# Seven block products in the first feed-forward, PSUM tiles of their own, and modulation columns spread over the stages

## The chip, the core and the metric

The kernel runs on one core of a Trainium2 chip. The metric is the device time of one execution in microseconds; the time of a kernel is the median of its runs. Engines are named as in the profile: PE is TensorE (matmuls), DVE is VectorE, ACT is ScalarE, POOL is GpSimd, and SP is the engine that issues most transfers.

## The reference

Two layers over 512 tokens of 1024 channels. Layer 0 mixes with a Fourier transform and a windowed attention, layer 1 with pooled averages. Each layer ends with a gated feed-forward of 22 x 128 = 2816 hidden units, and six modulation vectors of 1024 (shift, scale and gate of the mixer and of the feed-forward) come from the condition c.

```python
def ada_mod(cond, w, b):
    m = jax.nn.silu(cond) @ w + b
    return jnp.split(m[..., None, :], 6, axis=-1)

def swiglu(h, w1, w3, w2):
    return (jax.nn.silu(h @ w1) * (h @ w3)) @ w2

def reference(x, c, ctx, ...):
    h, hc = x, ctx
    for layer in range(DEPTH):
        sh1, sc1, g1, sh2, sc2, g2 = ada_mod(c, ada_w[layer], ada_b[layer])
        ...
        xn = modulate(rms_norm(h, norm_mix_g[layer]), sh1, sc1)
        y = even_mixer(...) if layer % 2 == 0 else pool_mix(...)
        h = h + g1 * y
        hn = modulate(rms_norm(h, norm_ffn_g[layer]), sh2, sc2)
        h = h + g2 * swiglu(hn, ffn_w1[layer], ffn_w3[layer], ffn_w2[layer])
    return rms_norm(h, final_g)
```

Everything is fp32.

## The kernel before

**Products.** A fp32 product is made from halves: each operand is split into a rounded high part and the rest, and `passes` issues three matmuls: high x high, low x high, high x low. The weights' high part is a copy on ScalarE (`w_h`, line 67 is the helper of all its operations), the low part a subtraction on VectorE (`w_l`, L155). `Stream` (`ws`) keeps the weights in order: a raw piece of 128 x 1024 (512 KB) is loaded by SP into one of four `raw` buffers, and split some pieces ahead of its use.

**A feed-forward** (`ffn`, once for each layer). The hidden units are 22 tiles of 128, in groups of 8, 8 and 6 (`GROUPS`). A tile gives `av`, the product of the activated half and the other half, which is then split into `ah` and `al`. After each group come 8 output chunks: chunk `dt` multiplies the group's tiles with a piece of w2 in a PSUM bank `w2_ps` of the pool `mm`, and VectorE adds it, gated, to `h`. Tile 0 of each feed-forward is made ahead of it (`Lead`).

**An ordinary tile** takes two weight pieces and gives 8 x 2 x 3 = 48 matmuls of 512 columns into a two-bank tile `h_ps` of the pool `ss`, which has two such tiles.

**A block tile** (`Quarters`) computes the same as a 2 x 2 product of blocks with seven block products instead of eight, by the Winograd form of Strassen's scheme: 7 x 4 x 3 = 84 matmuls of 256 columns. The stationary sides are the raw block a1 (`w_r`), the sums s12 and s34 (`s_f`, made by VectorE with adds of 512 columns) and a22; each is split into halves. The moving sides are the blocks of the normed input and four combinations `t`, made once for a feed-forward in `pieces`. A product is named by its moving side (b11, t1, t2, t3, b21, t4, b22). Products are summed in four quarters of 256 columns, r[0] to r[3], of one two-bank `h_ps` tile; several products add to the same quarter. After four products VectorE makes `x`, `v` and part of `c_q`; after all seven, one add of 512 columns (L986) reads two quarters of the tile at once into `c_q`, and `av` follows. `first` and `second` prepare the next tile's weights inside the present tile. The low part of a22 is made differently from the others: ScalarE writes the negative of the high part, and a GpSimd transfer adds the raw weights from memory to it (L939, 256 KB, `accum_op`).

Before, `QUARTERED` has no tile of the first feed-forward and tiles 4 to 21 of the second.

**Modulation columns.** A column of a modulation vector is a dot product of 128 x 1024 weights with the condition: SP loads 512 KB (`ada_r`, L212) into a buffer of the same `raw` ring as the weights, and VectorE multiplies and sums it (L219). `acol1` has 56 of them left for the first feed-forward: the gate columns of its own layer and all of the second layer. Three are made after each tile from tile 2 on.

**What sets the order.** The Tile framework's scheduler orders the instructions of each engine from the program's order and from when their inputs should be there. So what is written after a group can be issued before its end. Each engine then runs its list in order, waiting on semaphores. The eight PSUM banks are: `mm` 3, `fl` 1, `ss` 2 x 2.

## Time and profile before

| | before |
|---|---|
| median of 3 runs | 1002.17 us (1000.08 to 1002.96) |
| profiled execution | 998.42 us |
| its span | 996.6 us |
| mean granted TensorE clock | 0.995 |
| TensorE busy | 960.5 us in 5464 matmuls |
| VectorE busy | 679.7 us |
| ScalarE busy | 428.1 us |
| GpSimd busy | 42.4 us |

The profile is of one execution. Times in the trace count from the start of its span; the first feed-forward lies at some 250 to 600 us, the second at some 640 to 983 us. A row of a windows view gives a stretch, its length, and the busy time and number of instructions of each engine in it. A row of a timeline gives start, length, engine, line, output and inputs, and in brackets how long the engine was idle before it and what ended that. Small differences between the median and the profiled execution are the usual ones between executions of one program.

### The profile page before, as it was taken

How to read it: one execution, taken by the hardware profiler on the slowest of the kernel's cores; microseconds unless marked ns; L12 is line 12 of the kernel's file. 1: busy time of each engine (PE TensorE's matmuls, PEld its weight loads, DVE VectorE, ACT ScalarE, POOL GpSimd, SP SyncE). 2: the span in 40 equal slices, each digit the busy share in tenths (PEclk: the TensorE clock that was granted, in tenths of full speed). 3: DMA queues.
4: the chain of work that ended last, by engine and by line, in shares of the span. 5: the costliest groups of instructions: out<-in, count | busy, mean ns of one | idle time of the engine just before them, and what ended most of it. 6: DMA issues, size and time to landing. Idle time of an engine off the chain costs nothing.

```text
span 996.6 us, 13925 instructions
## 1 busy us (share of the span) xinstructions
PE 960.5 (96%) x5464; PEld 800.5 (80%) x5464; DVE 679.7 (68%) x1086; ACT 428.1 (43%) x689; POOL 42.4 (4%) x45
## 2 busy tenths in 40 slices
PE   4999999999999999999999999999999999999995
PEld 3766767676888888888888888789989999889984
DVE  5678577879867455565456398898565885657654
ACT  4568565454532222232223355654432544315531
POOL 1011011011000000000000001000000100000000
PEclk9999999999999999999999999999999999999997
DMA  9931211753577446665365323133441444413412
GB/s 338 345 106 32 106 48 64 237 182 127 188 256 256 165 149 213 221 219 189 109 219 197 118 105 103 33 92 99 143 144 43 141 124 138 148 43 109 114 32 85
DMA packets 47009, 143.98 MB, mean 144 GB/s; under 512 B 5728, under 2 KB 5856, under 8 KB 46944
## 3 DMA queue, kind: packets, MB, share of 16 engines
q1 hardware_dynamic: 44352, 138.38, 40.9%
q0 software_dynamic: 2592, 4.72, 2.9%
q8 instruction: 43, 0.70, 0.3%
q14 instruction: 22, 0.18, 0.0%
HBM read 140.98 MB, written 2.10 MB: 144 GB/s over the span
## 4 chain that ended last, share of the span: by engine, by line
PE 84%; DVE 9%; ACT 4%; issue 2%; DMA 0%; DVEq 0%; SPq 0%; ACTq 0%
PE h_ps L180 14%; PE h_ps L181 14%; PE h_ps L182 14%; PE w_ps L180 8%; PE w_ps L182 8%; PE w_ps L181 8%; PE pv_ps L757 2%; ACT w_h L67 2%; DVE w_l L155 2%; PE t_ps L746 2%; PE mo_ps L180 1%; PE mo_ps L182 1%; PE mo_ps L181 1%; PE s_ps L709 1%; PE s_cx L422 1%
## 5 line engine op out<-in xcount | busy, mean ns | idle before, releaser
L67 ACT ACTIVATE w_h<-w_r 128x1024 fp32r<-128x1024 f32 (+2 forms) x158 | 148.0, 942 | 276.4 <-PE h_ps L182 154.5
L180 PE MATMUL h_ps<-hnh,w_h 128*128 128x512 f32 (+1 forms) x600 | 212.0, 353 | 3.0 <-DVE c_q L986 2.9
L181 PE MATMUL h_ps<-hnh,w_l 128*128 128x512 f32 (+1 forms) x600 | 210.5, 351 | 0.4 <-DVE w_l L155 0.4
L182 PE MATMUL h_ps<-hnl,w_h 128*128 128x512 f32 (+1 forms) x600 | 210.5, 351 | 0.0
L155 DVE TENSOR_TENSOR w_l<-w_r,w_h 128x1024 fp32r<-128x1024 f32 (+2 forms) x140 | 158.6, 1137 | 57.8 <-ACT w_h L67 57.2
L219 DVE SCALAR_TENSOR_TENSOR ada_r<-ada_r,condB 128x1024 f32<-128x1024 f32 x80 | 97.5, 1221 | 69.4 <-DMA ada_r<-in_adaR_dram 68.9
L180 PE MATMUL w_ps<-ah,w_h 128*128 128x512 f32 x352 | 137.5, 391 | 0.0
L181 PE MATMUL w_ps<-ah,w_l 128*128 128x512 f32 x352 | 137.0, 389 | 0.0
L182 PE MATMUL w_ps<-al,w_h 128*128 128x512 f32 x352 | 136.8, 390 | 0.0
L180 PEld LDWEIGHTS h_ps<-hnh,w_h 128*128 128x128 f32 x600 | 113.3, 189 | 20.6 <-DVE c_q L986 4.8
L181 PEld LDWEIGHTS h_ps<-hnh,w_l 128*128 128x128 f32 x600 | 113.4, 189 | 15.9 <-DVE w_l L155 0.8
L182 PEld LDWEIGHTS h_ps<-hnl,w_h 128*128 128x128 f32 x600 | 113.4, 189 | 14.9
L1052 DVE SCALAR_TENSOR_TENSOR h<-w_ps,ada,h 128x512 f32<-128x512 f32 x48 | 35.7, 749 | 67.8 <-PE w_ps L182 67.8
L181 PE MATMUL h_ps<-t_h,w_l 128*128 128x256 f32 x288 | 81.5, 283 | 0.0
L180 PE MATMUL h_ps<-t_h,w_h 128*128 128x256 f32 x288 | 81.5, 283 | 0.0
L182 PE MATMUL h_ps<-t_l,w_h 128*128 128x256 f32 x288 | 81.5, 283 | 0.0
L180 PEld LDWEIGHTS w_ps<-ah,w_h 128*128 128x128 f32 x352 | 66.1, 188 | 14.7 <-ACT ah L67 1.3
L182 PEld LDWEIGHTS w_ps<-al,w_h 128*128 128x128 f32 x352 | 66.1, 188 | 14.2 <-DVE al L1031 0.6
L181 PEld LDWEIGHTS w_ps<-ah,w_l 128*128 128x128 f32 x352 | 66.1, 188 | 13.3
L67 ACT ACTIVATE w_h<-s_f 128x1024 fp32r<-128x1024 f32 x36 | 38.0, 1056 | 55.0 <-PE w_ps L182 31.5
L67 ACT ACTIVATE ah<-av 128x512 fp32r<-128x512 f32 x44 | 27.8, 632 | 67.4 <-DVE av L1028 47.4
L155 DVE TENSOR_TENSOR w_l<-s_f,w_h 128x1024 fp32r<-128x1024 f32 x36 | 44.1, 1225 | 17.3 <-ACT w_h L67 17.0
(271 smaller groups left out, 1536.3 us busy)
## 6 DMA issues: line engine op xcount, KB each, us to landing
w_r<-in_w_dram SPq DMA_DIRECT2D x88, 512.0 KB, 3.6
ada_r<-in_adaR_dram SPq DMA_DIRECT2D x80, 512.0 KB, 4.2
w_r<-in_w2a_dram SPq DMA_DIRECT2D x32, 512.0 KB, 4.2
ada_q<-in_adaP_dram SPq DMA_DIRECT2D x32, 256.0 KB, 5.7
w_r<-in_w2b_dram SPq DMA_DIRECT2D x16, 384.0 KB, 3.0
w_l<-in_w_dram POOLq DMA_DIRECT2D x18, 256.0 KB, 5.5
w_r<-in_wo_dram SPq DMA_DIRECT2D x16, 256.0 KB, 2.9
wa_r<-in_wa_dram SPq DMA_DIRECT2D x8, 384.0 KB, 6.0
```

Source lines behind the costliest of these rows:

```text
L67: return nc.scalar.activation(out=out, in_=in_, func=func, **kw)
L155: nc.vector.tensor_tensor(lo, src, f32(hi), op=ALU.subtract)
L180: nc.tensor.matmul(acc, wh, mh, start=start, stop=False, skip_group_check=shared)
L181: nc.tensor.matmul(acc, wl, mh, start=False, stop=False, skip_group_check=shared)
L182: nc.tensor.matmul(acc, wh, ml, start=False, stop=stop, skip_group_check=shared)
L219: nc.vector.scalar_tensor_tensor(out=r, in0=r, scalar=1.0, in1=condB, op0=ALU.mult, op1=ALU.mult, accum_out=ada[l][:, t:t + 1])
L422: nc.tensor.matmul(ps[32 * g:32 * g + 32, :], condS[:, kt, :], r[:, k * n:(k + 1) * n], start=(kt < 4), stop=(kt >= 4), tile_position=(0, ...
L709: nc.tensor.matmul(sp[:, c:c + n], q, KH[kv][:, k0:k0 + n], start=True, stop=False)
L746: nc.tensor.transpose(tp[:, c * P:(c + 1) * P], Ps[c][:, n * P:(n + 1) * P], ident)
L757: nc.tensor.matmul(ops[64 * kv:64 * kv + 64, 0:256], VS[:, kbs[n], kv, :], th[:, 256 * kv:256 * kv + 256], start=(n == 0), stop=(n == N - ...
L1052: nc.vector.scalar_tensor_tensor(out=h[:, dt, :], in0=acc, scalar=ada[l][:, 40 + dt:41 + dt], in1=h[:, dt, :], op0=ALU.mult, op1=ALU.add)
```

## The change

Four things are changed together.

1. *Which tiles.* Tiles 6 to 21 of the first feed-forward become block tiles too. Tiles 4 to 21 of the second stay block tiles.
2. *PSUM and order on TensorE.* For the block tiles of a feed-forward the pool `ss` is closed and four one-bank tiles `q0` to `q3` (pool `sq`) take its banks, each holding one 256-column result. The same products as before add to the same quarter (b11 and b21, t1 and b22, t3 and t4), in the order b11, t1, t2, b21, t3, b22, t4; each first result is read before the second product goes into its bank. VectorE's one wide add becomes two of 256 columns. TensorE keeps the order that the program is written in, through the whole feed-forward (`manual_schedule`).
3. *Preparation.* It is cut into three steps and spread over two tiles (`prepare`, `step`). The low part of a1 is no longer split by VectorE but made as a22's is: a negative copy by ScalarE and a GpSimd accumulation, here of 512 KB (`low`).
4. *Modulation columns.* They are spread over nearly all tiles (one or two each) and the output chunks of the first two groups (two each). From tile 5 on, a tile's own columns load into a single buffer `adar`, and so does every second one of the chunks' (`alone`).

Beside these the ring of activation halves has 16 buffers instead of 17 (`NA`), and the final norm uses `rstd_short`, which takes the reciprocal of 128 x 4 values and spreads them afterwards.

```diff
-QUARTERED = (frozenset(), frozenset(range(4, NHID)))
-NA = 17
+QUARTERED = (frozenset(range(6, NHID)), frozenset(range(4, NHID)))
+NA = 16
...
-                self.raw.append(raw_tile(1024, "ada_r"))
+                self.raw.append(pf.tile([P, 1024], F32, tag="adar", bufs=1, name="ada_r") if self.alone
+                                else raw_tile(1024, "ada_r"))
...
+        def rstd_short(self):
+            rs = self.rstd_cols()
+            bc = mm.tile([P, 512], F32, tag="mm", name="bc_ps")
+            for b in range(self.n // P):
+                nc.tensor.matmul(bc[:, b * P:(b + 1) * P], rs[:, b:b + 1].broadcast_to([P, P]), ident, start=True,
+                                 stop=True)
+            return bc
...
+        def low(self, hi, lo, src, dram):
+            act(hi, src)
+            act(lo, f32(hi), scale=-1.0)
+            nc.gpsimd.dma_start(out=lo, in_=dram, accum_op=ALU.add)
+            return hi, lo
+
+        def prepare(self):
+            d1, d3 = [u[0] for u in ws.units[len(ws.ready):len(ws.ready) + 2]]
             r1, r3 = ws.take(2)
+            n = dict(a1=self.low(*ws.slots_for(1024), r1, d1))
+            self.ahead.append(n)
+            yield
             s12 = ...
-            n = dict(r1=r1, r3=r3, f=s12, s12=ws.split(s12), a1=ws.split(r1))
+            n["s12"] = ws.split(s12)
+            yield
+            s34 = ...
+            n["a22"] = self.low(hi, lo, r3[:, 512:1024], d3[:, 512:1024])
+            n["s34"] = ws.split(s34)
+            yield
...
-            hp = ss.tile([P, 1024], F32, tag="s", name="h_ps")
-            r = [hp[:, q * 256:(q + 1) * 256] for q in range(4)]
+            r = [self.ps.tile([P, 256], F32, tag=f"q{q}", bufs=1, name="h_ps") for q in range(4)]
             self.product(r[0], w["a1"], 0, "b11", start=True)
-            if more:
-                self.first()
+            act(x[:, q0], r[0])
+            if left > 0:
+                self.step(1)
             self.product(r[2], w["s12"], 0, "t1", start=True)
-            self.product(r[1], w["s12"], 512, "t2")
-            self.product(r[3], w["s34"], 0, "t3")
...
+            self.product(r[1], w["s12"], 512, "t2", start=True)
+            nc.vector.tensor_tensor(x[:, q1], x[:, q0], r[1], op=ALU.add)
+            nc.vector.tensor_tensor(y[:, q0], x[:, q1], r[2], op=ALU.add)
             self.product(r[0], w["a1"], 512, "b21")
+            act(si[:, q0], r[0], AF.Silu)
+            self.product(r[3], w["s34"], 0, "t3", start=True)
+            nc.vector.tensor_tensor(c[:, q1], y[:, q0], r[3], op=ALU.add)
+            if left > 0:
+                self.step(2)
+            if left > 1:
+                self.step(0)
+            self.product(r[2], w["s34"], 512, "b22")
+            nc.vector.tensor_tensor(y[:, q1], x[:, q1], r[2], op=ALU.add)
+            act(si[:, q1], y[:, q1], AF.Silu)
             self.product(r[3], w["a22"], 0, "t4")
-            nc.vector.tensor_tensor(c[:, 0:512].rearrange("p (a b) -> p a b", a=2),
-                                    x[:, 256:512].unsqueeze(1).broadcast_to([P, 2, 256]),
-                                    hp[:, 512:1024].rearrange("p (a b) -> p a b", a=2), op=ALU.add)
...
+            nc.vector.tensor_tensor(c[:, q0], x[:, q1], r[3], op=ALU.add)
...
+        if quartered:
+            order.enter_context(tc.manual_schedule(engines={PE}))
...
-                if l == 0 and j > 1:
-                    for _ in range(3):
+                if l == 0 and j > 0:
+                    acol1.alone = j + 1 >= quartered[0]
+                    for _ in range(2 if 2 < j < quartered[0] else 1):
                         acol1.step()
...
+                if l == 0 and gi < 2:
+                    for n in range(2):
+                        acol1.alone = n == 1 or dt == KT - 1
+                        acol1.step()
...
-        rstd = ffn(1, rstd, Af1, lead, pool=pt8).rstd()
+    rstd = ffn(1, rstd, Af1, lead).rstd_short()
```

What the order of instructions becomes is seen at three places. On VectorE, in the second group of the first feed-forward, before (an ordinary tile; `ada_r` is the modulation weights' buffer, `w_r` a raw weight piece):

```order
L219 SCALAR_TENSOR_TENSOR ada_r,ada_107<-ada_r,condB 128x1024 x3
L155 TENSOR_TENSOR w_l<-w_r,w_h 128x1024
L1028 TENSOR_TENSOR av<-si,h_ps 128x512
L155 TENSOR_TENSOR w_l<-w_r,w_h 128x1024
L1031 TENSOR_TENSOR al<-av,ah 128x512
```

A tile has two splits, two operations on its result and three columns in a row. At the same place after, in tile 11 (a block tile):

```order
L1000 TENSOR_TENSOR y<-x,h_ps 128x256
L953 TENSOR_TENSOR s_f<-w_r 128x512
L1004 TENSOR_TENSOR c_q<-y,h_ps 128x256
L954 TENSOR_TENSOR s_f<-s_f,w_r 128x512
L223 SCALAR_TENSOR_TENSOR ada_r,ada_107<-ada_r,condB 128x1024
L1010 TENSOR_TENSOR y<-x,h_ps 128x256
L153 TENSOR_TENSOR w_l<-s_f,w_h 128x1024
L1013 TENSOR_TENSOR c_q<-x,h_ps 128x256
L958 TENSOR_TENSOR s_f<-w_r 128x512
L1015 TENSOR_TENSOR av<-si,c_q 128x512
L959 TENSOR_TENSOR s_f<-w_r,s_f 128x512
L223 SCALAR_TENSOR_TENSOR ada_r,ada_107<-ada_r,condB 128x1024
```

Two columns now stand between the adds that read PSUM and those that prepare weights; one of the two was written behind an output chunk of this group, and the scheduler moved it forward. VectorE's list has 25 columns in tiles 6 to 15 and none in tiles 16 to 21.

On SP, which issues the loads, in the second group of the first feed-forward, before:

```order
L212 DMA ada_r<-in_adaR_dram 128x1024 x3
L136 DMA w_r<-in_w_dram 128x1024 x2
L212 DMA ada_r<-in_adaR_dram 128x1024 x3
L136 DMA w_r<-in_w_dram 128x1024 x2
L212 DMA ada_r<-in_adaR_dram 128x1024 x3
```

and after, in the same group:

```order
L216 DMA ada_r<-in_adaR_dram 128x1024
L137 DMA w_r<-in_w_dram 128x1024
L216 DMA ada_r<-in_adaR_dram 128x1024
L137 DMA w_r<-in_w_dram 128x1024
L216 DMA ada_r<-in_adaR_dram 128x1024
```

Column and weight loads alternate one for one, where three and two stood together.

On TensorE, in the second feed-forward, before, where one block tile gives way to another (the numbers are those of buffers: `h_ps_6840` is one tile's pair of banks, `h_ps_6969` another's, `hnh` and `hnl` the halves of the normed input):

```order
L180 MATMUL h_ps_6840<-t_h_5751,w_h_6786 128x256
L181 MATMUL h_ps_6840<-t_h_5751,w_l_6788 128x256
L182 MATMUL h_ps_6840<-t_l_5753,w_h_6786 128x256
L180 MATMUL h_ps_6969<-hnh_5625,w_h_6860 128x256
L181 MATMUL h_ps_6969<-hnh_5625,w_l_6862 128x256
L182 MATMUL h_ps_6969<-hnl_5626,w_h_6860 128x256
```

After, in the same feed-forward, where each number is one bank:

```order
L183 MATMUL h_ps_7181<-t_h_7003,w_h_7127 128x256
L184 MATMUL h_ps_7181<-t_h_7003,w_l_7128 128x256
L185 MATMUL h_ps_7181<-t_l_7005,w_h_7127 128x256
L183 MATMUL h_ps_7312<-hnh_6718,w_h_7136 128x256
L184 MATMUL h_ps_7312<-hnh_6718,w_l_7137 128x256
L185 MATMUL h_ps_7312<-hnl_6719,w_h_7136 128x256
```

Before, the scheduler put the first product of a later tile in between, while the earlier tile still had products to come; after, a tile's seven products follow each other as they are written.

More of the change, by code (lines that the diff above doesn't have):

```diff
@@ L63 @@
     fl = ctx.enter_context(tc.tile_pool(name="fl", bufs=1, space=PSUM))
-    ss = ctx.enter_context(tc.tile_pool(name="ss", bufs=2, space=PSUM))
+    wide = ExitStack()
+    ss = wide.enter_context(tc.tile_pool(name="ss", bufs=2, space=PSUM))
     def act(out, in_, func=AF.Copy, **kw):
@@ L881 @@
     stage = ExitStack()
-    pq = stage.enter_context(tc.tile_pool(name="pq", bufs=1))
+    pq = bh = bl = None
     alt["pool"] = pf
@@ L956, in product, with run @@
                 s_ = slice(c0 + k * P, c0 + k * P + P)
-                passes(acc, [x[:, s_] for x in w], self.moving(m, k), start and k == 0, k == 3, not start)
-        def run(self, more):
-            w = self.next
+                passes(acc, [x[:, s_] for x in w], self.moving(m, k), start and k == 0, k == 3, True)
+        def run(self, left):
+            w = self.ahead.pop(0)
             ws.skip(2)
-            hp = ss.tile([P, 1024], F32, tag="s", name="h_ps")
-            r = [hp[:, q * 256:(q + 1) * 256] for q in range(4)]
+            r = [self.ps.tile([P, 256], F32, tag=f"q{q}", bufs=1, name="h_ps") for q in range(4)]
+            x, y, si, c = sf("x"), sf("y"), sf("si"), sf("c_q")
+            q0, q1 = slice(0, 256), slice(256, 512)
             self.product(r[0], w["a1"], 0, "b11", start=True)
-            if more:
-                self.first()
+            act(x[:, q0], r[0])
+            if left > 0:
+                self.step(1)
             else:
@@ L992, in run, with ffn @@
             return av
-    def ffn(l, rstd, A, lead, each=None, pool=None):
+    def ffn(l, rstd, A, lead, each=None, then=None):
+        nonlocal ss
+        phase = ExitStack()
+        pool = phase.enter_context(tc.tile_pool(name="pt8", bufs=1, reuse_waits="tile"))
         nrm = Norm(pf, T)
@@ L1015, in ffn @@
                 elif j in quartered:
-                    av = quarters.run(j + 1 in quartered and j + 1 < j0 + nj)
+                    if j == quartered[0]:
+                        wide.close()
+                        quarters.ps = narrow.enter_context(tc.tile_pool(name="sq", bufs=1, space=PSUM,
+                                                                        reuse_waits="tile"))
+                    av = quarters.run(j0 + nj - 1 - j)
                 else:
@@ L1057, in ffn, with pool_stage @@
                         each(dt)
+        order.close()
+        if quartered:
+            narrow.close()
+            ss = wide.enter_context(tc.tile_pool(name="ss", bufs=2, space=PSUM, reuse_waits="tile"))
         return nrm
     xs, A1, PX = [], [], []
-    bh = pq.tile([P, 4, 536], F32R, tag="bh", bufs=1, name="bh")
-    bl = pq.tile([P, 4, 40], F32R, tag="bl", bufs=1, name="bl")
+    def pool_stage():
+        nonlocal pq, bh, bl
+        pq = stage.enter_context(tc.tile_pool(name="pq", bufs=1, reuse_waits="tile"))
+        bh = pq.tile([P, 4, 536], F32R, tag="bh", bufs=1, name="bh")
+        bl = pq.tile([P, 4, 40], F32R, tag="bl", bufs=1, name="bl")
     def pool_band_load(g):
@@ L1165 @@
     stage.close()
-    with tc.tile_pool(name="pt8", bufs=1, reuse_waits="tile") as pt8:
-        rstd = ffn(1, rstd, Af1, lead, pool=pt8).rstd()
+    rstd = ffn(1, rstd, Af1, lead).rstd_short()
+    wide.close()
     for kt in range(KT):
```

71 lines of the change are left out of this document (30 added, 41 removed).

## The prediction

> **What bounds the kernel now.** I read the page's head first, then the chain that ended last, then each stage by windows, then the waits of TensorE and VectorE.
>
> ```profile
> span 996.6 us, 13925 instructions
> PE 960.5 (96%) x5464; PEld 800.5 (80%) x5464; DVE 679.7 (68%) x1086; ACT 428.1 (43%) x689; POOL 42.4 (4%) x45
> PE 84%; DVE 9%; ACT 4%; issue 2%; DMA 0%; DVEq 0%; SPq 0%; ACTq 0%
> ```
>
> TensorE (PE) is busy 96% of the span and is 84% of the chain; no transfer stands in the chain. So time is won by issuing less on TensorE, and lost where another engine makes it wait. The next view gives four stretches: eight ordinary tiles of the first feed-forward, one block tile, and two stretches of block tiles in the second.
>
> ```profile
> core 0: us, PE busy (x) PEld busy (x) DVE busy (x) ACT busy (x) POOL busy (x), PEclk, DMA share, GB/s
> 370.39:457.43 87.04, 87.04 (x386) 72.07 (x384) 53.18 (x78) 23.38 (x30) 0.00 (x0) 1.00 0.66 217
> 702.07:712.22 10.15, 10.15 (x85) 10.15 (x85) 5.79 (x9) 4.10 (x9) 0.00 (x0) 1.00 0.48 142
> 759.43:828.96 69.53, 67.48 (x553) 66.55 (x552) 52.74 (x76) 35.08 (x54) 4.59 (x6) 1.00 0.38 104
> 887.22:934.91 47.69, 46.80 (x386) 46.28 (x385) 34.56 (x50) 23.47 (x36) 2.87 (x4) 1.00 0.33 88
> ```
>
> The first row is 8 tiles without a gap: 87.04 / 8 = 10.88 us for 48 matmuls of 512 columns, 0.2267 each. The second has 84 of 256 columns at the step that the next rows show, 0.12 us: 84 x 0.12 = 10.06 us (the window holds one more). The third and fourth should take 552 x 0.12 = 66.1 and 384 x 0.12 = 46.0, and take 3.4 and 1.7 longer. The timeline shows one such loss, the waits view their releaser:
>
> ```profile
> 795.71 0.28 PE L180 MATMUL h_ps<-t_h,w_h 128*128 128x256 f32 x1
> 795.83 0.28 PE L181 MATMUL h_ps<-t_h,w_l 128*128 128x256 f32 x1
> 795.95 0.28 PE L182 MATMUL h_ps<-t_l,w_h 128*128 128x256 f32 x1
> 796.21 0.69 DVE L986 TENSOR_TENSOR c_q<-x,h_ps 128x512 f32<-128x512 f32 x1 [0.37 <-ACT si L67]
> 796.95 0.39 PE L180 MATMUL h_ps<-hnh,w_h 128*128 128x256 f32 x1 [0.72 <-DVE c_q L986]
> PE h_ps L180 <- DVE c_q L986: 2.9, 6, 0.7
> ```
>
> Starts go 0.12 apart, then 1.00: the first product of another tile waits until VectorE has read the bank pair that it goes to.
>
> **The change part by part.**
>
> *Block form in tiles 6 to 21 of the first feed-forward.* 16 x (10.88 - 10.06) = **-13.1 us**, on the path, since those stretches hold TensorE alone. [...]
>
> *Own banks and written order.* No product now goes into a bank that a wider read holds; the add of c_q is cut into two 256-column adds, and at least one product (t3 to t4: b22) lies between a result and the next product into its bank. The two windows lost 3.4 + 1.7 = 5.1. I take **-4.6**: half a microsecond stays, because the first block tile of a layer must wait for the last reader of the wide banks. Ends: 0 (each wait returns in another place) and -5.5 (with the shorter stretch of tiles ahead of these windows).
>
> *Short final norm.*
>
> ```profile
> 984.27 0.42 PE L272 MATMUL nrm_ps<-sq,ones 128*32 128x128 f32 x8 [1.15 <-ACT sq L67]
> 984.77 0.37 ACT L67 ACTIVATE std<-nrm_ps,eps 128x128 f32<-128x128 f32 x1 [0.55 <-PE nrm_ps L272]
> 985.17 0.95 DVE L278 RECIPROCAL rs<-std 128x128 f32<-128x128 f32 x1 [1.61 <-ACT std L67]
> 601.60 0.95 PE L258 MATMUL nrm_ps<-ones,sq 128*128 128x1 f32 x8
> 602.58 0.26 ACT L67 ACTIVATE std<-nrm_ps,eps 128x4 f32<-128x4 f32 x1 [1.33 <-PE nrm_ps L258]
> 602.88 0.18 DVE L263 RECIPROCAL rs<-std 128x4 f32<-128x4 f32 x1
> ```
>
> The short form stands in the other norm: reciprocal -0.77, root -0.11, sums 0.95 - 0.42 = +0.53: **-0.4**, all on the chain. Ends 0 and -0.9.
>
> *VectorE in a block tile.* The rows of one stretch of block tiles, and two splits back to back:
>
> ```profile
> L155 DVE TENSOR_TENSOR w_l<-s_f,w_h 128x1024 fp32r<-128x1024 f32 x12 | 14.7, 1225 | 8.4 <-ACT w_h L67 8.4
> L942 DVE TENSOR_TENSOR s_f<-w_r 128x512 f32<-128x512 f32 x6 | 4.1, 684 | 0.0
> L974 DVE TENSOR_TENSOR x<-x,h_ps 128x256 f32<-128x256 f32 x6 | 2.5, 414 | 0.0
> 599.82 2.35 DVE L155 TENSOR_TENSOR w_l<-w_r,w_h 128x1024 fp32r<-128x1024 f32 x2
> ```
>
> Two of 1.22 took 2.35, so back to back each is 0.08 shorter. A block tile has 2 splits x 1.14, 4 half-width adds and the two of av and al x 0.60, 5 narrow adds x 0.33: 7.55 us. In the second feed-forward that is all, against 10.06: 2.5 us free, hence I cost the two extra narrow adds at nothing there. The split of a1 leaves VectorE.
>
> *Columns.* In the first feed-forward there are the modulation columns as well, and the order has 25 of them in tiles 6 to 15: two in each of 8 to 13, three or four in 6, 7, 14 and 15, none in 16 to 21.
>
> ```profile
> L219 DVE SCALAR_TENSOR_TENSOR ada_r<-ada_r,condB 128x1024 f32<-128x1024 f32 x21 | 25.7, 1225 | 32.1 <-DMA ada_r<-in_adaR_dram 31.8
> ada_r<-in_adaR_dram SPq DMA_DIRECT2D x56, 512.0 KB, 4.4
> ada_r<-in_adaR_dram SPq DMA_DIRECT2D x3, 512.0 KB, 3.5
> w_r<-in_w_dram SPq DMA_DIRECT2D x2, 512.0 KB, 6.9
> ```
>
> (The last three: transfers of 250 to 600 us, of 356 to 363 with nothing beside them, and of 730 to 732 beside an accumulation.) Two columns add 2 x 1.15: 9.85 of 10.06, so VectorE fits only if it never waits. It does wait now, 31.8 us for 21 columns. That is hidden, because an ordinary tile gives VectorE little else: with those waits it fills 53.18 + 32.1 of 87.04 us. In tiles 8 to 13 all columns use one buffer: column, issue, landing, next column. That loop is 1.22 + 4.4 = 5.6 us, two are 11.2 per tile against 10.06. VectorE works in order, so a column that waits for its load holds up the adds that read the PSUM banks, and TensorE waits at the next product into them. The weight loads stand in SP's queue between the column loads, one for one, and come at the loop's pace too, two per tile, behind a stock of two tiles, the four raw buffers, which are theirs alone once the columns have their own. So 1.2 us per tile for 10 tiles, 12, less what TensorE can be late unseen: one product of 12 x 0.12 = 1.44 us lies between a result and the next product into its bank, some 2 us with the split-ahead, in each of two runs of tiles (6 and 7, 8 to 15): **+8**. The lower end is 0: at the 3.5 us of an idle queue two loops are 9.4. The upper is 25 x 1.5 (31.8 / 21) = 38, if every wait comes through. I stand by 4.4, since it is the median of 56 such transfers in this very stage.
>
> *Low parts by accumulation.* 34 tiles with 512 + 256 KB each, where 18 had 256 KB; the source view of that line, then its row in the 730 to 732 view:
>
> ```profile
> L939 POOL DMA_DIRECT2D w_l<-in_w_dram x18: 856/865/1011, 635.2 to 934.6; - x18
> DMA to landing us min/median/max: 3.9/5.5/7.2
> w_l<-in_w_dram POOLq DMA_DIRECT2D x1, 256.0 KB, 7.2
> ```
>
> GpSimd needs 2 x 0.87 us a tile, behind which nothing is queued. The 512 KB piece is begun in the tile before last, so even twice 5.5 us is hidden. The a22 piece is issued, by its place on ScalarE's queue, some 11.7 us after the start of the tile ahead of its use, and used by the last product, 10.06 + 72 x 0.12 = 18.7: 7.0 us for 5.5. I cost it at nothing.
>
> *ScalarE* gains the negative copies: four 1024-wide, three of half that and three narrow ones.
>
> ```profile
> L67 ACT ACTIVATE w_h<-s_f 128x1024 fp32r<-128x1024 f32 x36 | 38.0, 1056 | 55.0 <-PE w_ps L182 31.5
> L1052 DVE SCALAR_TENSOR_TENSOR h<-w_ps,ada,h 128x512 f32<-128x512 f32 x48 | 35.7, 749 | 67.8 <-PE w_ps L182 67.8
> 249.95:326.87 76.92, 76.54 (x339) 63.07 (x338) 56.79 (x80) 29.12 (x39) 0.00 (x0) 1.00 0.70 239
> ```
>
> At 1.06 for the wide ones, in proportion for the others, some 7.3 of 10.06 us: nothing. In the output chunks of the first two groups (8 tiles x 3 passes = 24 matmuls, 24 x 0.2267 = 5.4 us) VectorE has 0.75 + 1.14 + 2 x 1.15 = 4.2: nothing. The pieces of the normed input, some 11 us of VectorE (16 half-width of 0.6 at most, 4 of 1.14 less overlap), lie in tiles 1 to 5, where the last row has VectorE at 56.79 of 76.92 us with the three columns a tile that move away: nothing, at most 2. The ring of activation halves loses one of 17 buffers; eight tiles hold two each, so the first of the next group is written after the last output chunk has read its predecessor, which it does by program order anyway: nothing.
>
> Sum: -13.1 - 4.6 - 0.4 + 8 = **-10.1**. The profiled execution took 998.42 us (span 996.6), the median of the runs is 1002.17: 988.3 against the first, **992** against the median.
>
> **The rivals.** *All hidden.* Columns land in 3.5 and the slack takes the rest: -18.1, 984. For it: 3.5 was seen, and the own buffer is held by nothing but the column before. Against: it was seen with the queue empty, and the DMA share is 0.66 in the first window, with one tile's transfers about to grow.
>
> *Transfers get in each other's way.* The queue rows of the page:
>
> ```profile
> q1 hardware_dynamic: 44352, 138.38, 40.9%
> q0 software_dynamic: 2592, 4.72, 2.9%
> ```
>
> At 100% of the 16 engines these are 138.38 / (0.409 x 996.6) = 340 GB/s and 163. A tile with two columns and two weight pieces (2.1 MB, 6.2 us) and 0.79 MB accumulated (4.8 us) needs 11.0 us of 10.06. If one load in three tiles lands in 6.9 rather than 4.4, that is 0.8 us a tile, 8 in ten tiles: about 1000. [...]
>
> *Slower: the a22 accumulation is late in every block tile.* It has 7.0 us and, so far alone, took up to 7.2. Behind 512 KB more on the same queue an average of 7.3 would cost 34 x 0.3 = 10 us and eat the gain; at 8.0 it is +34, 1026. Against it: the 512 KB piece goes out most of a tile earlier, and layer 1 has 2 x 512 KB of loads a tile, 3.1 + 4.8 = 7.9 of 10.06.
> [...]
>
> **How the numbers follow.** The forecast (988 to 996) has 0.43, all hidden 0.25, transfers in each other's way (996 to 1004) 0.22, the late accumulation 0.10. What a measurement tells from no change is 0.3%, 3 us. Faster (under 999.2) is 0.25 + 0.43 + 0.12 of the third = 0.80; same 0.10 + 0.02; slower 0.08. The range 983 to 1001 leaves out the lower edge of the second case, the upper third of the third and the last.
>
> **What would show it.** Windows over tiles 16 to 21 of the first feed-forward should be 6 x 10.06 = 60.4 us (6 x 10.88 = 65.3 before), over 8 to 15 some 85 to 86, where 80.5 is ideal; TensorE's waits there should name adds released late by the column line, whose own wait for its load should be over 1 us each. In the second feed-forward no wait on c_q and 10.06 to 10.1 a tile. Wrong if tiles 8 to 15 are near 80.5 (columns hidden) or over 90 (transfers), or if TensorE waits for a low part of w in the last product of a tile.

## The result, and the profile after

The changed kernel takes 1026.21 us (median of 4 runs, 1025.81 to 1028.35) where the kernel before takes 1001.22: a ratio of 1.0255 (95% interval 1.024 to 1.0271). It was forecast 10 us faster and is 25 us slower. The profiled execution took 1028.35 us, 29.9 more than that of before, and the lines below are of that one. The page of after first: head, busy times, queues, and the chain by engine.

```profile
span 1026.6 us, 15558 instructions
PE 959.9 (94%) x6040; PEld 829.4 (81%) x6040; DVE 744.2 (72%) x1251; ACT 516.5 (50%) x807; POOL 85.9 (8%) x95
q1 hardware_dynamic: 44352, 138.38, 40.1%
q0 software_dynamic: 9792, 26.74, 15.3%
PE 50%; DMA 11%; DVE 8%; issue 3%; ACT 1%; DVEq 0%; ACTq 0%; SPq 0%
```

TensorE is busy as long as before (959.9 and 960.5 us), although sixteen tiles push an eighth fewer columns, so it ran slower for a time, and it stood still for 67 us where it stood for 36. Transfers, which had no share of the chain, have 11%. Windows over the first feed-forward tell where: the first group's tiles 1 to 7, its output chunks, tiles 8 to 15, tiles 16 to 21; then tiles 16 to 21 of the second.

```profile
core 0: us, PE busy (x) PEld busy (x) DVE busy (x) ACT busy (x) POOL busy (x), PEclk, DMA share, GB/s
252.89:344.15 91.26, 79.81 (x409) 68.75 (x410) 76.23 (x118) 43.71 (x57) 3.64 (x4) 0.91 0.65 201
344.15:387.69 43.54, 43.54 (x194) 36.06 (x193) 29.64 (x47) 12.73 (x15) 3.45 (x4) 1.00 0.85 261
387.69:494.53 106.84, 87.21 (x674) 85.92 (x673) 83.46 (x138) 51.17 (x73) 10.43 (x12) 0.90 0.77 218
538.17:599.55 61.38, 60.87 (x505) 60.57 (x504) 46.37 (x74) 37.16 (x55) 6.96 (x8) 1.00 0.58 140
919.17:979.65 60.48, 60.48 (x506) 60.47 (x505) 43.69 (x69) 36.96 (x54) 6.95 (x8) 1.00 0.58 140
```

Where no columns stand beside them, block tiles take what was promised: 60.48 / 6 = 10.08 us. Tiles 8 to 15 take 106.84 us where 80.5 was ideal and 87.04 was the time before. The whole first feed-forward, from its first own product to its last output chunk (252.89 to 632.22), takes 379.33 us where before took 348.92 (249.95 to 598.87) and the block form alone promised 348.92 - 13.1 = 335.8. That is 43.5 us more than promised. Who is waited for, first on TensorE, then on VectorE:

```profile
PE h_ps L183 <- DVE y L1000: 18.6, 5, 10.6
PE h_ps L183 <- DVE av L1062: 10.4, 2, 9.5
PE h_ps L183 <- DVE c_q L1004: 2.3, 4, 1.4
DVE ada_r L223 <- DMA ada_r<-in_adaR_dram: 56.2, 34, 6.2
DVE s_f L953 <- DMA w_r<-in_w_dram: 7.4, 6, 2.5
```

TensorE waits for VectorE's reads of PSUM (y, av, c_q); VectorE waits for column loads. The timeline shows one such wait from end to end, at the change from wide banks to narrow ones:

```profile
313.61 0.69 DVE L959 TENSOR_TENSOR s_f<-w_r,s_f 128x512 f32<-128x512 f32 x1
320.47 1.23 DVE L223 SCALAR_TENSOR_TENSOR ada_r<-ada_r,condB 128x1024 f32<-128x1024 f32 x1 [6.17 <-DMA ada_r<-in_adaR_dram]
321.62 0.68 DVE L1062 TENSOR_TENSOR av<-si,h_ps 128x512 f32<-128x512 f32 x1
322.36 0.58 PE L183 MATMUL h_ps<-t_h,w_h 128*128 128x256 f32 x1 [9.49 <-DVE av L1062]
```

The operation av is the last reader of the wide banks. It stands behind a column in VectorE's queue; that column waits 6.17 us for its load, and TensorE 9.49 us for av. What follows is slow too. Two windows, right behind this wait and behind the longest one, in tile 8:

```profile
322.36:325.29 2.93, 2.93 (x13) 2.93 (x14) 2.84 (x4) 0.89 (x2) 0.00 (x0) 0.50 0.52 179
405.69:410.40 4.71, 4.71 (x22) 4.71 (x23) 4.28 (x7) 1.36 (x2) 0.00 (x0) 0.50 0.86 272
```

The granted clock is 0.50 (the seventh figure), and a matmul of 256 columns takes 0.21 us instead of 0.12. In the first feed-forward 60 matmuls of 256 columns start 0.21 us apart and 12 of 512 columns 0.43: 60 x 0.09 + 12 x 0.20 = 7.8 us. With 33.4 us of waits, from start to start less the step, summed over the gaps of more than 0.3 us, that is 41.2 of the 43.5.

The second feed-forward, from its first own product to the final norm, of before and of after, and the tail of after:

```profile
642.09:982.70 340.61, 337.60 (x2187) 307.37 (x2186) 234.20 (x327) 146.75 (x214) 14.75 (x17) 1.00 0.34 100
675.46:1012.32 336.86, 335.30 (x2187) 307.99 (x2187) 220.69 (x327) 169.48 (x232) 30.45 (x35) 1.00 0.52 129
1013.98 1.17 PE L262 MATMUL nrm_ps<-ones,sq 128*128 128x1 f32 x8 [0.72 <-ACT sq L68]
1015.71 2.08 PE L275 MATMUL bc_ps<-ident,rs 128*128 128x128 f32 x8 [0.57 <-DVE rs L267]
```

It gained 3.75 us. The tail lost some: from the end of the output chunks to the first output operation it was 982.70 to 987.87, now 1012.32 to 1017.83, +0.3. The last section shows that the granted clock makes this difference, and not the short norm.

### The profile page after: what moved, and what is told of

Read it like the earlier page. It is cut to its first block, busy times and chain, and to the rows that moved or that the text cites. A ratio compares the mean times of both kernels' runs of the same rounds, so it can differ in the third digit from the quotient of the medians.

```text
span 1026.6 us, 15558 instructions
## 1 busy us (share of the span) xinstructions
PE 959.9 (94%) x6040; PEld 829.4 (81%) x6040; DVE 744.2 (72%) x1251; ACT 516.5 (50%) x807; POOL 85.9 (8%) x95
## 4 chain that ended last, share of the span: by engine, by line
PE 50%; DMA 11%; DVE 8%; issue 3%; ACT 1%; DVEq 0%; ACTq 0%; SPq 0%
PE h_ps L183 10%; PE h_ps L184 10%; PE h_ps L185 10%; DMA ada_r<-in_adaR_dram 9%; PE w_ps L185 6%; PE w_ps L184 6%; PE w_ps L183 6%; DVE ada_r L223 3%; DMA w_r<-in_w_dram 2%; DVE w_l L153 1%; ACT w_h L68 1%; DVE fo L1223 0%; DVE t_l L934 0%; DVE t_f L929 0%; DVE al L1065 0%
## 5 line engine op out<-in xcount | busy, mean ns | idle before, releaser
L183 PE MATMUL h_ps<-hnh,w_h 128*128 128x256 f32 (+1 forms) x536 | 168.7, 315 | 20.5 <-DVE y L1000 18.6
L183 PE MATMUL h_ps<-t_h,w_h 128*128 128x256 f32 x544 | 157.0, 289 | 13.7 <-DVE av L1062 10.4
L185 PE MATMUL h_ps<-hnl,w_h 128*128 128x256 f32 (+1 forms) x536 | 167.9, 313 | 0.8 <-DVE hnl L367 0.8
L184 PE MATMUL h_ps<-hnh,w_l 128*128 128x256 f32 (+1 forms) x536 | 167.6, 313 | 0.0
L184 PE MATMUL h_ps<-t_h,w_l 128*128 128x256 f32 x544 | 155.5, 286 | 0.0
L185 PE MATMUL h_ps<-t_l,w_h 128*128 128x256 f32 x544 | 155.5, 286 | 0.0
L223 DVE SCALAR_TENSOR_TENSOR ada_r<-ada_r,condB 128x1024 f32<-128x1024 f32 x80 | 97.7, 1223 | 56.5 <-DMA ada_r<-in_adaR_dram 56.2
L183 PEld LDWEIGHTS h_ps<-t_h,w_h 128*128 128x128 f32 x544 | 106.3, 195 | 15.7 <-DVE av L1062 10.8
L153 DVE TENSOR_TENSOR w_l<-w_r,w_h 128x1024 fp32r<-128x1024 f32 (+2 forms) x90 | 97.9, 1092 | 14.0 <-ACT w_h L68 12.3
L184 PEld LDWEIGHTS h_ps<-t_h,w_l 128*128 128x128 f32 x544 | 106.3, 195 | 0.0
L185 PEld LDWEIGHTS h_ps<-t_l,w_h 128*128 128x128 f32 x544 | 106.0, 195 | 0.0
L185 PEld LDWEIGHTS w_ps<-al,w_h 128*128 128x128 f32 x352 | 66.1, 188 | 13.9 <-DVE al L1065 0.2
```

Source lines behind the costliest of these rows:

```text
L153: nc.vector.tensor_tensor(lo, src, f32(hi), op=ALU.subtract)
L183: nc.tensor.matmul(acc, wh, mh, start=start, stop=False, skip_group_check=shared)
L184: nc.tensor.matmul(acc, wl, mh, start=False, stop=False, skip_group_check=shared)
L185: nc.tensor.matmul(acc, wh, ml, start=False, stop=stop, skip_group_check=shared)
L223: nc.vector.scalar_tensor_tensor(out=r, in0=r, scalar=1.0, in1=condB, op0=ALU.mult, op1=ALU.mult, accum_out=ada[l][:, t:t + 1])
```

## The experiments

Each was timed beside the kernel before on the same chip. "First" is the length of the first feed-forward in the profile, with its tiles 8 to 15 apart; in before, second_only and the four kernels whose names begin with third these are ordinary tiles, in all others block tiles. The kernels no_loads, loads_unread and no_accumulation leave out loads, their use, or accumulations, so they do not compute the reference.

| kernel | median us | ratio to before (95%) | first | tiles 8 to 15 |
|---|---|---|---|---|
| before | 1000.1 to 1001.5 | | 348.9 | 87.0 |
| after | 1026.2 | 1.024 to 1.027 | 379.3 | 106.8 |
| second_only | 998.3 | 0.996 to 0.999 | 349.0 | 87.0 |
| no_loads | 993.6 | 0.990 to 0.995 | 342.8 | 81.0 |
| alternate | 1017.5 | 1.013 to 1.020 | 365.7 | 95.8 |
| written_order | 1083.9 | 1.079 to 1.085 | 430.1 | 121.0 |
| own_input_buffers | 1028.0 | 1.021 to 1.030 | 382.6 | 106.7 |
| low_on_dve | 1012.0 | 1.006 to 1.014 | 364.2 | 90.3 |
| tab1 | 1024.2 | 1.017 to 1.026 | 377.2 | 90.5 |
| tab2 | 1024.6 | 1.018 to 1.027 | 375.2 | 92.5 |
| loads_unread | 1029.6 | 1.027 to 1.031 | 364.9 | 98.1 |
| no_accumulation | 1011.5 | 1.008 to 1.012 | 362.3 | 93.3 |
| third_only | 1011.1 | 1.008 to 1.012 | 361.7 | 87.0 |
| loads_by_pool | 1036.0 | 1.034 to 1.043 | 383.4 | 110.7 |
| third_lazy2 | 1001.9 | 1.000 to 1.003 | 351.0 | 87.0 |
| full3 | 1023.1 | 1.019 to 1.025 | 367.6 | 92.3 |
| full4 | 1010.8 | 1.009 to 1.013 | 359.4 | 86.7 |
| third_a | 1000.6 | 0.998 to 1.000 | 355.3 | 87.0 |
| third_d | 998.2 | 0.995 to 0.999 | 347.5 | 87.0 |

**second_only: the second feed-forward's part alone.**

```diff
-QUARTERED = (frozenset(range(6, NHID)), frozenset(range(4, NHID)))
+QUARTERED = (frozenset(), frozenset(range(4, NHID)))
...
+                if l == 0 and j > 1:
+                    for _ in range(3):
+                        acol1.step()
```

> The first feed-forward has ordinary tiles again, with three columns after each tile from tile 2 on; the second keeps its own banks, written order and accumulated low parts, and the short final norm stays. Theory A (all of the loss lies in the first feed-forward, where VectorE waits for column loads): 997 to 999 us, some 3 us under before, since the second feed-forward took 336.9 us where it took 340.6. Rival (the written order or the accumulations cost something outside the first feed-forward too): 1001 us or more.

998.26 us, ratio 0.9974, as theory A had it: 0.3% faster than before, and far faster than after. Own banks, written order on TensorE, the accumulated low parts of a1 and the short norm are worth that much together; the run does not tell them apart. The first feed-forward takes 349.0 us again, so the loss is all in its part of the change.

**no_loads: columns without their loads.**

```diff
-                nc.sync.dma_start(out=self.raw[-1], in_=adaR[48 * l + t])
+                if not self.bare:
+                    nc.sync.dma_start(out=self.raw[-1], in_=adaR[48 * l + t])
...  in0=condB if self.bare else r
```

> As after, but the 56 modulation columns of the first feed-forward are computed from the condition itself, without their loads: VectorE's work and order stay, the 56 transfers of 512 KB are left out. Theory A (VectorE stands still in its queue for the column loads): the stalls go, 985 to 990 us. Rival C (VectorE's own work, 9.85 us of a tile's 10.06, is too much): tiles 8 to 15 still take over 95 us and the time stays above 1010.

993.64 us, some 4 more than expected. Its windows over tiles 1 to 7 and 8 to 15:

```profile
252.76:334.29 81.53, 78.47 (x408) 67.32 (x409) 78.86 (x124) 43.49 (x57) 3.64 (x4) 0.96 0.43 123
377.84:458.87 81.03, 80.89 (x674) 80.69 (x672) 73.99 (x126) 51.93 (x74) 10.42 (x12) 1.00 0.69 158
```

Tiles 8 to 15 take 81.03 us of the ideal 80.5, and without the loads the stage is 379.3 - 342.8 = 36.5 of the 43.5 us shorter. But VectorE's order did not stay as it was: the scheduler moved columns forward, so that the first four stretches (tiles 1 to 7, chunks, tiles 8 to 15, chunks) have 19, 20, 13 and 4 columns where after has 15, 11, 19 and 11. The 36.5 us are therefore the price of the loads together with the order that goes with them. For the same reason this window, with VectorE 91% busy, does not settle rival C; the trace of after does, where the work of 83.46 us is 3 us over the ideal of a window that is 26.3 over it (rival C falls as the main cause). The other 7 us are in the first window: at its start 1.3 us of waits and 11 matmuls of 512 columns at 0.43 us (2.2), then waits of 1.6 and 1.2 at the change of banks.

**own_input_buffers: the start of the stage.**

```diff
-            us.append(sf("nrm_u", tag="a", bufs=NA) if quartered else None)
+            us.append((pb.tile([P, T], F32, tag="tmp", bufs=8, name="nrm_u") if l == 0 else
+                       sf("nrm_u", tag="a", bufs=NA)) if quartered else None)
```

> As after, but the eight normed inputs of the first feed-forward (nrm_u) lie in the pool that they lay in before, not in the ring of activation halves, whose first buffers are memory of the stage ahead. In after TensorE waited 2.3 us for the first of them, 1.3 us more on the next, and then ran 17 matmuls of 512 columns at 0.43 instead of 0.23 us: 1.96 + 1.3 + 3.4 = 6.7 us. Theory D (that wait and its slow matmuls are a cost of their own): 1018 to 1021. Rival (the later stalls are set by column loads that would then only be waited for longer): 1025 to 1028.

1028.03 us, in the rival's range. The wait at the start went (0.11 us between the lead's last matmul and the first own product, instead of 2.08), but eight buffers of a ring that others use were now held until the pieces were made, and TensorE waited there:

```profile
PE h_ps L183 <- DVE z L349: 8.4, 1, 8.4
```

So it does not price the wait by itself. In the kernels that make these inputs from the halves later (third_lazy2, third_a, third_d) tiles 1 to 7 take 76.92 us, as before: that form has no wait at the start.

**alternate and loads_by_pool: the one buffer, and the queue in front of it.**

```diff
-                self.raw.append(pf.tile(..., tag="adar", ...) if self.alone
+                self.raw.append(pf.tile(..., tag="adar", ...) if self.alone and len(self.raw) % 2
```

> As after, but every second one of the columns that went through the single buffer goes through the ring of four raw buffers instead. Theory A with the single buffer as the cause (column, issue, landing, next column): the loop has two loads under way, so waits on loads fall to a third and the time to 1000 to 1008 us. Rival B (the 16 DMA engines are crowded by loads and accumulations, so that a load lands in 6 to 10 us whatever its buffer): 1018 to 1027.

1017.48: between the two theories. VectorE's waits for columns fell from 56.2 to 32.5 us, but those for weights rose from 7.4 to 18.6 (the raw ring was now shared), and 13.6 us came back. The order changed here too: tiles 8 to 15 have 8 columns instead of 19, so the 13.6 us are not the price of the buffer alone.

```diff
-                nc.sync.dma_start(out=self.raw[-1], in_=adaR[48 * l + t])
+                (nc.gpsimd if self.alone else nc.sync).dma_start(out=self.raw[-1], in_=adaR[48 * l + t])
```

> As after, but the column loads into the single buffer are issued by GpSimd instead of SP, so that the weight loads no longer stand behind them in SP's queue; the accumulations now do, in GpSimd's. In the kernel whose column loads nobody read, SP issued five column loads one after the other's landing and VectorE waited 13.0 us for a weight load behind them. Theory E (SP's queue standing behind the one buffer is what starves VectorE): weights come in time, 1000 to 1012 us. If VectorE's own waits for columns and the crowded engines are the cause, the queue does not matter: 1020 to 1032.

1036.00, over both ranges. The columns stand where they stood, and with SP's queue free of these loads VectorE waited less for weights (4.0 us instead of 7.4); but it waited 62.7 us for columns, more than in after, and the accumulations now stood behind them. Theory E, SP's queue as the main cause, falls for this kernel, though the new queue has a price of its own that the run does not separate.

**loads_unread: the loads run, nobody reads them.**

```diff
-            nc.vector.scalar_tensor_tensor(out=r, in0=r, ...
+            nc.vector.scalar_tensor_tensor(out=junk if self.bare else r, in0=condB if self.bare else r, ...
```

> As after, but the 56 columns of the first feed-forward are computed from the condition itself while their loads still run, into the same buffers, with no reader: the traffic stays, VectorE never waits for a column (the columns are not the reference's). With the kernel without these loads at 993.6 us it splits the loss. Theory A (VectorE standing still behind columns): 990 to 998 us. Rival B (crowded DMA engines delay weights and accumulations too, which TensorE then waits for): 1008 to 1020.

1029.59, outside both ranges; but the time is not comparable as a whole: 41 of the columns, free of their loads, ran ahead in the mixer, which ended 13.9 us later (the first feed-forward's first product stands at 266.78 instead of 252.89). The first feed-forward itself, now almost without column work on VectorE, took 364.9: 14.4 less than after, yet 22 more than without the loads. So the loads cost though nobody waits for a column. One wait of TensorE of 12.3 us is the queue's. SP's rows, then VectorE's:

```profile
397.82 18.66 SPq L218 DMA_DIRECT2D ada_r<-in_adaR_dram  x5
416.58 0.37 SPq L137 DMA_DIRECT2D w_r<-in_w_dram  x1
426.84 0.69 DVE L955 TENSOR_TENSOR s_f<-w_r 128x512 f32<-128x512 f32 x1 [13.04 <-DMA w_r<-in_w_dram]
```

Five column loads, each waiting for the landing of the one before in the single buffer, held SP for 18.7 us, and a weight load behind them came 13 us late. So the one buffer costs on SP's queue too, when loads bunch.

**no_accumulation and low_on_dve: what the 512 KB accumulations do.**

```diff
-            n = dict(a1=self.low(*ws.slots_for(1024), r1, d1))
+            n = dict(a1=self.low(*ws.slots_for(1024), r1, d1, self.l == 1))     # no transfer in the first
```

> As after, but the 16 accumulations of 512 KB of the first feed-forward are left out, with nothing in their place (a1's low part there is only the negative of its high part); VectorE's work is that of after. Theory A with landings that the accumulations lengthen (columns land sooner without them, so VectorE waits less): 1005 to 1015 us. If it is the one-buffer loop alone, whatever runs beside it: 1022 to 1028.

1011.50, as expected of landings that the accumulations lengthen: 14.7 us less than after, 17.0 in the first feed-forward, with the columns where they were but for one. From 298 to 498 us columns landed in 4.4 us and weights in 4.5; VectorE's waits for columns in the stage fell from 51.0 to 37.0 us.

```diff
+            n = dict(a1=ws.split(r1) if self.l == 0 else self.low(*ws.slots_for(1024), r1, d1))
```

> As after, but in the first feed-forward the low part of a1 is split by VectorE again, so that the 16 accumulations of 512 KB there go; each block tile gives VectorE a split of 1.14 us more. Theory A (VectorE's queue stands still behind columns): no gain, 1024 to 1035. Rival B (the DMA engines are crowded by the accumulations): 1008 to 1018.

1011.99: rival B's number, although VectorE has 16 splits more (here too the order moved: 13 columns in tiles 8 to 15). In after, columns landed in 4.6 us (before: 4.1) and weights in 5.2 (3.6), from 298 to 498 us; here are its two queues:

```profile
q1 hardware_dynamic: 10768, 39.23, 57.1%
q0 software_dynamic: 2880, 7.87, 22.5%
ada_r<-in_adaR_dram SPq DMA_DIRECT2D x41, 512.0 KB, 4.6
w_r<-in_w_dram SPq DMA_DIRECT2D x18, 512.0 KB, 5.2
```

The accumulations take 22.5% of the engines' time for 7.87 MB, the loads 57.1% for 39.23.

**written_order: VectorE in the order as written.**

```diff
-            order.enter_context(tc.manual_schedule(engines={PE}))
+            order.enter_context(tc.manual_schedule(engines={PE, DVE} if l == 0 else {PE}))
```

> As after, but VectorE too keeps the order in which the program is written, through the first feed-forward: one column a tile, behind the tile's last operation, and two behind each output chunk, none pulled forward. The transfers are the same ones. Theory A: a column's load has a tile's 10 us to land, tiles 8 to 15 take 81 to 84 us; with some 4 us lost where the wide banks are given back, 986 to 994 us. Rival B (crowded DMA engines): still over 1010.

1083.91, the worst, against both expectations. Its last six tiles take 89 us, though VectorE waits only 5.1 us for columns in them:

```profile
562.29:651.35 89.06, 67.87 (x505) 66.36 (x504) 60.16 (x97) 40.19 (x59) 8.74 (x10) 0.89 0.66 177
PE h_ps L183 <- DVE y L1000: 18.1, 5, 10.5
```

As written, the weights' sums and splits of the next tile stand ahead of the adds that read PSUM, and the splits wait 13.5 us for ScalarE in this window. It is no test of the columns; it shows that the columns are not the only waits in VectorE's queue that can reach TensorE.

**tab1 and tab2: columns moved out of most block tiles.**

```diff
-                    for _ in range(2 if 2 < j < quartered[0] else 1):
+                    for _ in range([1, 2, 2, 2, 2, 1, 0, 1, 1, ...][j]):     # tab2: 2, 3, 3, 3, 2, 0, 0, 0, ...
```

> As after with the normed inputs in the pool of before, the weights of the first block tile prepared a tile earlier, and the columns dealt out anew: block tiles 8 to 13 and 16 to 21 get none in VectorE's order, tiles 1 to 5, 6, 7, 14 and 15 and the output chunks of two groups (two each) get all; the columns written behind chunks use the ring of four raw buffers. Theory A: tiles 8 to 13 take 10.06 us each; the time is 986 to 994 us. Rival B (the loads of a chunk, two columns and weights, crowd the DMA engines wherever they stand): TensorE waits in or just behind the chunks instead, 998 or more.

> As tab1, with other numbers: three columns a tile in tiles 1 to 3, one behind each chunk of the first group instead of two, one each in tiles 8 to 14 and two in 16 to 19 as written. Theory A: as tab1, 986 to 994 us. Rival B: less crowded in the first group's chunks, so 2 to 8 us under tab1.

1024.21 and 1024.61, far over theory A. Tiles 8 to 15 fell to 90.5 and 92.5 us, but both carry the inputs of own_input_buffers (8.9 and 10.7 us of waiting for z), and the bank switch waited 10.4 and 7.6 us for av behind columns. The gain in one place was lost in another, and rival B's 2 to 8 us between the two did not show.

**full3 and full4: the columns spread thinner, with and without accumulations.**

```diff
+                if l == 0 or j < 4:
+                    for _ in range([3, 3, 3, 3, 3, 1, 1, 1, ...][j] if l == 0 else 2):
+                        acol1.step()
```

> Block tiles in 6 to 21 as in after, with the columns spread thinner (three a tile in tiles 0 to 4, one from tile 5 on, one behind each chunk of two groups, eight in the second feed-forward), the single buffer only for the block tiles' own, normed inputs from the halves, the first block tile's weights a tile earlier. The accumulations stay. If single-buffer loop and column waits are the cause: 990 to 998. If the accumulations' crowding is: 1005 to 1020.

> As full3, with a1's low part split by VectorE in the first feed-forward, so without the 16 accumulations of 512 KB. Beside full3 it is the price of the accumulations where VectorE's columns are out of the way: if they crowd the column and weight loads, 8 to 15 us less than full3; if not, 0 to 5 us more.

1023.06, over both ranges, and 1010.79: without the accumulations 12 us less, as expected of crowding. Even so tiles 1 to 7 take 94.3 and 91.0 us where 5 x 10.88 + 2 x 10.06 = 74.5 would do, with VectorE busy 84.44 and 85.03 of them. There its work alone is some 10 us too much: columns, pieces, inputs and splits in seven tiles. In after it is 76.23 in that window, over 74.5 too.

**third_only, third_lazy2, third_a, third_d: block tiles in the third group only.**

```diff
+QUARTERED = (frozenset(range(16, NHID)), frozenset(range(4, NHID)))
...  # columns by tile, third_a: 0, 3, 3, 3, 3, 3, 2, 0, eight times 3, then 2, 2, 2, 2, 1, 1
...  # third_d: the last six 1, 1, 1, 1, 1, 0, and one a tile in tiles 0 to 7 of the second feed-forward
```

> Block tiles in the first feed-forward only in the third group (16 to 21), where VectorE's order has no columns: three columns a tile in tiles 2 to 15 and one behind each chunk of the first two groups, all in the ring of four raw buffers; the pieces of the normed input are made in tiles 4 to 7. The second feed-forward as in after. Theory A: 998.3 (the kernel with the second feed-forward's part alone) - 6 x 0.82 = 993.4, with a bank switch of some 1 us: 992 to 996. Rival (block tiles in the first feed-forward cost more than they save, columns or not): 998 or more.

> Block tiles in the first feed-forward only in the third group. Columns in the ring of four: three a tile up to tile 13, one a tile in 16 to 21, eight (the second layer's last gate) in the second feed-forward's tiles 0 to 3. The normed inputs for the pieces are made from the halves in tile 3 (as halves plus and minus the shift), in buffers that lie where after's do, so that the start of the stage waits for nothing. If a block tile without crowded loads saves what it promised: 998.3 - 6 x 0.82 = 993.4, some 1 us for the switch of banks: 992 to 996. If block tiles there cost more than they save: 998 or more.

> Block tiles in the first feed-forward in the third group only, as in the kernel before it of that kind, whose losses were 5.3 us in the first group's chunks (VectorE behind on three columns pulled into tile 7) and 2.3 us from columns in the second feed-forward. Here tile 7 gets no column, no chunk of the first group either; three a tile in 1 to 5 and 8 to 15, five in the second group's last chunks, one or two in tiles 16 to 21, none in the second feed-forward. If columns beside block tiles are what costs: tiles 16 to 21 lose up to 5 us with ten columns there, 994 to 1000. If nothing else is wrong and they are hidden: 993 to 995.

> As third_a, but only one column a tile in 16 to 20, two in the second group's chunks, and eight in the second feed-forward, one a tile in its tiles 0 to 7. Theory: one column a block tile is hidden (VectorE 7.55 + 1.15 + a wait of about 1.1 = 9.8 of 10.06): 998.3 - 4.9 + 1.5 (switch of banks) = 994 to 996.

third_only (1011.08) carries the inputs of own_input_buffers (6.8 us for z) and lost 8.3 us in chunks; third_lazy2 (1001.89) lost 5.3 us in the first group's chunks and 2.3 in the second feed-forward; both came out as their rival had it, 998 or more. third_a (1000.63) is just over its wider range, third_d (998.21) 2 us over its own. They differ mainly in the columns beside six block tiles. Their windows over tiles 16 to 21, each with its column row:

```profile
503.76:574.23 70.47, 64.21 (x506) 63.40 (x505) 51.22 (x86) 36.62 (x55) 6.94 (x8) 0.95 0.68 175
L223 DVE SCALAR_TENSOR_TENSOR ada_r<-ada_r,condB 128x1024 f32<-128x1024 f32 x7 | 8.6, 1222 | 6.7 <-DMA ada_r<-in_adaR_dram 6.7
503.69:565.67 61.98, 60.98 (x506) 60.71 (x505) 47.23 (x79) 36.66 (x55) 6.94 (x8) 1.00 0.69 170
L223 DVE SCALAR_TENSOR_TENSOR ada_r<-ada_r,condB 128x1024 f32<-128x1024 f32 x4 | 4.9, 1221 | 0.3 <-DMA ada_r<-in_adaR_dram 0.3
```

Seven columns that waited 6.7 us made these tiles 8.5 us longer than four that waited 0.3, at nearly the same share of the DMA engines and with VectorE busy only 51.22 of 70.47 us. That is the mechanism nearly alone: VectorE waits 6.7 us for columns, TensorE waits 6.3 for VectorE's reads of PSUM, so the wait passes on nearly whole, and the slow clock comes on top (0.95 granted on average in this window, 27 matmuls at 0.21). In third_d's profile the first feed-forward gained 1.4 us on before; the mixer of layer 1, where two of its columns ended up, gave back 3.3, and the second feed-forward, with five, gained 1.2 instead of 3.75. Its median is 0.997 of before. So second_only and third_d beat both kernels, by 0.3%, and no version that loads its columns and has block tiles in 6 to 15 did.

## Why the prediction was wrong, step by step

- *Block form, -13.1.* Right where nothing else comes in: 10.08 us a tile in after's last window, 61.38 for tiles 16 to 21 (60.4 was forecast), 81.03 for eight in no_loads.
- *Own banks and order, -4.6.* Measured -3.75 in the second feed-forward, where the waits for c_q fell from 2.9 to 0.4 us. Half a microsecond was left for the change of banks; it cost 1.06 there, and 9.49 in the first, where av stands behind a column. That place was named, its price not asked in the stage with columns.
- *Short norm, -0.4.* Measured +0.3, by the bad luck of the clock. The reciprocal shrank to 0.18 us as read off and the second sums took 1.17 instead of 0.42 (0.95 was read off); spreading the result took 2.08 instead of 1.66, but at a lower clock. In full3, whose clock falls at the same point of the spreading as in before, the tail is 4.98 us against 5.17: -0.2.
- *Columns, +8.* This is the term that failed. The loop of 5.6 us was compared with the tile, as if it ran beside VectorE's other work; two columns a tile were priced, 20 where 25 had been counted; and then 2 us were taken off in each run of tiles. But VectorE is one queue: work and waits add. In tiles 8 to 15 of after:

```profile
L223 DVE SCALAR_TENSOR_TENSOR ada_r<-ada_r,condB 128x1024 f32<-128x1024 f32 x19 | 23.3, 1224 | 21.8 <-DMA ada_r<-in_adaR_dram 21.7
```

  83.46 us busy and 21.7 waiting are 105.2 of the window's 106.84: 26.3 us over the ideal, where 5 were forecast. A column waited 21.7 / 19 = 1.14 us, less than the 1.5 of the kernel before; there it was hidden, here it is TensorE's. Work alone was also over: 83.46 is more than 80.5, since the tiles with three columns were counted as if they had two. The upper end that was written down, 25 x 1.5 = 38, lies near the 36.5 us that leaving out the loads gave back, but by luck: it was meant for tiles 6 to 15 alone, and the 36.5 hold losses at the change of banks and in tiles 1 to 7 as well.
- *Output chunks, "nothing".* Wrong by omission: VectorE was busy 29.64 us in the first group's chunks and waited 11.1 more for columns, 40.7 of 43.54, and went into tile 8 late. TensorE's 10.6 us wait, the longest for y, is in tile 8.
- *Pieces, "nothing, at most 2".* In tiles 1 to 7 VectorE was busy 76.23 us where TensorE needs 74.5, beside 8.7 us of waits for columns from 299 us on. There was no room for the pieces, since the columns had not moved away: 15 still stand in these tiles, where before had 19.
- *The ring with one buffer less, "nothing".* The normed inputs moved to that ring with the block form, and the first buffer came free only after the lead's last product. TensorE waited 2.0 us longer ahead of the stage (that is beside the 43.5) and 1.3 in it, and ran 12 matmuls of 512 columns at 0.43 us, 2.4: some 6 in all. Where these inputs lie was not looked at.
- *Low parts by accumulation, "nothing".* Their landing was in time: no row in which TensorE waits for a low part in after (written_order and full3 have one each, 3.1 and 1.4 us). But they cost other loads: leaving out the 512 KB ones gave back 14.7 us.
- *The rivals.* The transfers in each other's way had a right mechanism with a price of 8, and the sign that was named for it, over 90 us in tiles 8 to 15, came. The late a22 did not come; that its 1026 is the measured time is chance. The loads, which SP issues, and the accumulations, which GpSimd issues, were in each other's way: with the 512 KB accumulations left out the first feed-forward was 17 us shorter, and from 298 to 498 us columns landed in 4.4 us instead of 4.6 and weights in 4.5 instead of 5.2. Issuing the column loads from GpSimd gained nothing (1036.0 us, after 1026.2).

What stays open is how the 36.5 us divide. The accumulations are worth 17.0 (no_accumulation), the one price here that was taken with the columns nearly in place. The 13.6 of alternate and the 14.4 of loads_unread are not prices of the one buffer and of VectorE's waits: in both the columns moved, in loads_unread 41 of them out of the stage. The three may overlap, and no run separates them further. Two own buffers for the columns were not tried.

## What to carry to other kernels

VectorE's one queue paid work plus waits here: 83.46 and 21.7 of the 106.84 us of tiles 8 to 15. Before shortening the engine that covers such a queue, add the queue's waits to its busy time and ask whether the sum still fits; a wait that was hidden can become the bound, as the columns' did (1.5 us each in before, hidden; 1.14 us each in after, and TensorE's). Where an instruction that waits for a transfer can stand ahead of one that frees a buffer of the bottleneck, put the second first or give the first its data early: at the change of banks a column's wait of 6.17 us stood ahead of av, and TensorE waited 9.49 us. And look at what a moved tile's buffers held before: the first write of the normed inputs waited here for the last reader of that memory, and TensorE waited 2.0 us longer ahead of the stage.

## What the runs showed of the hardware

In after TensorE's granted clock halved around its long waits. In the first feed-forward it is 0.50 in five stretches of the trace, 6.83, 10.24, 13.65, 3.41 and 3.41 us long, all whole multiples of 3.41 us, and a matmul of 256 columns starts every 0.21 us there instead of 0.12. Four lie at the waits of 2.65 us and more (at 1.38 us there was none), one at the start of the stage, where waits of 1.82 and 0.81 us have two matmuls between them. Behind such a wait TensorE ran 2.9 to 6 us at that clock, which added 7.8 us to 33.4 us of waits, a quarter more.

Where that clock falls can pass for the price of a change. Here are the tail's spreading matmuls, in before (the old form), full3, after and alternate (the short form):

```profile
986.17:987.84 1.67, 1.66 (x8) 1.36 (x8) 0.00 (x0) 0.00 (x0) 0.00 (x0) 0.65 0.00 0
1006.10:1007.80 1.70, 1.66 (x8) 1.36 (x8) 0.00 (x0) 0.00 (x0) 0.00 (x0) 0.65 0.00 0
1015.71:1017.79 2.08, 2.08 (x8) 1.78 (x8) 0.00 (x0) 0.00 (x0) 0.00 (x0) 0.50 0.00 0
1003.50:1004.70 1.20, 1.16 (x8) 0.97 (x8) 0.00 (x0) 0.00 (x0) 0.00 (x0) 1.00 0.00 0
```

At the same mean clock, 0.65, both forms take 1.66 us; the short form takes 2.08 at 0.50 and 1.16 at 1.00. The whole tail is 5.17, 4.98, 5.51 and 4.48 us in these four. The difference between after and before is when the clock fell: 0.94 us ahead of the spreading in after, 0.49 us into it in before.
